# A two-layer hybrid decoder in one kernel: six of the 22 gate/up pairs of each half FFN as whole products, the others as block products of an input that already holds 1/rms

## The chip, the cores and the metric

The kernel runs on one core of a Trainium2 chip. The metric is the device time of one execution in microseconds (us), the median of the runs that are given. TensorE (PE) does the matrix products, VectorE (DVE) and ScalarE (ACT) the element work, GpSimd (POOL) some of it, and the queue of SyncE (SP) issues nearly all transfers.

## The reference

Two layers over 512 tokens of width 1024, all in float32. Each layer is a half FFN, a mixer and another half FFN; the mixers (layer 0: latent attention and gated linear attention, layer 1: sparse attention) are not touched here. There are thus four half FFNs:

```
def rms_norm(x, g):
    y = xf * lax.rsqrt(jnp.mean(xf * xf, axis=-1, keepdims=True) + NORM_EPS)
    return (y * g.astype(jnp.float32)).astype(x.dtype)

def swiglu(x, w_gate, w_up, w_down):
    return (jax.nn.silu(x @ w_gate) * (x @ w_up)) @ w_down

h = h + 0.5 * swiglu(rms_norm(h, ffn_norm[layer, 0]), ffn_w_gate[layer, 0], ffn_w_up[layer, 0], ffn_w_down[layer, 0])
```

The hidden width is 2816, that is 22 blocks of 128. For each block one **pair** is to be made: 128 rows of the gate product and 128 rows of the up product, both over all 1024 input channels and 512 tokens.

## The kernel before

**Layout.** The residual lies transposed in SBUF as eight tiles `x0` to `x7` (the order listings call them x_79 to x_86), 128 channels by 512 tokens each. Every float32 operand of a product is split into a rounded high part and a low part (`split`, L149 to L151: a cast on ACT, a subtraction on DVE), and `mm3` (L143) makes a product of three matmuls: high by high, high by low, low by high (lines 145, 146, 147 of the profile, whatever the product).

**A pair by seven block products.** The channels are cut in two halves, the tokens in two halves of `H` = 256, and gate and up are the two row blocks: a 2 by 2 by 2 block product, made in Strassen's manner (Winograd's form) with seven products in place of eight. The price is in sums. `gate_up` (L113) loads the two weight blocks of 128 by 1024, makes four sums of 128 by 512 on DVE (`sa`, `sb`, L130 to L133) and splits the gate block, `sa`, `sb` and half of the up block. `ffn_input` (L254) makes the seven parts of the input once per half FFN: products of `x` with the gain, their sums (`xf`, L274), their high parts (`xh`, on ACT) and low parts (`xl`, L269, L279, L151 on DVE). 1/rms of each token is not in them. `gate_up_steps` (L302) issues the seven products as a generator, each 4 channel blocks by 3 matmuls of 256 columns, 84 matmuls for a pair; in between ACT and DVE copy and add parts out of PSUM. It ends with `done(gt, ut)`, which is `hidden` (L352): DVE multiplies `gt` by the broadcast tile `rb` of 1/rms (L354), GpSimd multiplies `ut` by it (L355), ACT applies Silu (L356), GpSimd makes the product (L357), ACT and DVE split it into `hid`.

**The order of a half FFN.** `ffn_body` (L343) first makes the input parts, then pairs 0 and 1 in step with each other; `rb` is asked for after their third step (`norm_stats`: squares on ACT, sums of the squares on DVE in the first half FFN and on GpSimd in the other three, L215; a matmul over partitions, L178; seven small DVE steps and a square root on ACT; the diagonal `dg`, L182; a matmul that spreads it, L184; a copy to `rb`, L167). Then the pairs follow one another. The down projection is done in groups of 5, 5, 4, 4 and 4 blocks: once a group's `hid` tiles exist, eight `unit`s (L362), one for each block of output channels, load a slice of `wd`, split it, multiply (`ps_d`) and add into `x` (L369). They are dealt out between the pairs of the next group; the last group's units end the half FFN.

**Buffers.** PSUM has 4 banks for gate/up (`gu`), 3 for the down projection and 1 for the statistics. Three raw weight tiles, three high/low pairs `whi`/`wlo` (gate blocks, `wd` slices) and three `shi`/`slo` (the sums) go round. The tag `act` has 14 tiles: the seven input parts, high and low. The tag `hid` has 9.

**What sets the order.** The program is written stage by stage, and a scheduler of the framework with a timing model of its own arranges each engine's instructions; each engine then runs its list in order and waits at its head. `tc.high_priority(AHEAD)` pulls the copies out of PSUM forward.

Of the kernel before, what the change touches and what calls it, by code (L numbers as in the profile page):

```python
# [19 lines left out]
P = 128  # L20
# [5 lines left out]
EPS = 1e-6  # L26
NEG = -1e30
TINY = 1e-30
GROUPS = ((0, 5), (5, 10), (10, 14), (14, 18), (18, 22))
H = T // 2  # L30
AHEAD = 400
HID = 9
# [6 lines left out]
class Core:  # L39


    def __init__(self, ctx, tc, a):
        self.ctx, self.tc, self.nc, self.a = ctx, tc, tc.nc, a
        nc = self.nc
        ep = lambda name, bufs, **k: ctx.enter_context(tc.tile_pool(name=name, bufs=bufs, **k))
        self.cp = ep("const", 1)
        self.xp = ep("resid", 1)
        self.sp = ep("scr", 1)
        self.wp = ep("wts", 1, side="right")
        cp = self.cp  # L50
# [12 lines left out]
        self.load_x(0, 2)  # L63
        nc.sync.dma_start(out=self.gains, in_=a["gains"])
        self.first = self.gate_up(0, 0, parts=2, meanwhile=lambda: self.load_x(2, KC))

    def load_x(self, k0, k1):
        for k in range(k0, k1):
# [34 lines left out]
        self.fws = ExitStack()  # L103
        self.fw = self.fws.enter_context(self.pool("sums", side="right"))

    def wload(self, src, n, keep=None):

        raw = self.raw(src, n)
        hi, lo = keep or self.wparts()
        self.split(raw[:, :n], hi[:, :n], lo[:, :n])  # L110
        return hi, lo

    def gate_up(self, f, j, parts=1, meanwhile=None):  # L113


        V, a = self.nc.vector, self.a
        w = T
        g = self.raw(a["wgu"][f, j, 0], 1024, parts)
        gh, gl = self.wparts()
        for i in range(parts):  # L120
            c = slice(i * 1024 // parts, (i + 1) * 1024 // parts)
            self.split(g[:, c], gh[:, c], gl[:, c])
        if meanwhile:
            meanwhile()
        u = self.raw(a["wgu"][f, j, 1], 1024)
        ah, al = self.sparts()
        bh, bl = self.sparts()
# [123 lines left out]
        pool, n = self.act  # L251
        return pool.tile([P, 4, H], R, name=name, tag="act", bufs=n)

    def ffn_input(self, gi, hp):  # L254


        V, S = self.nc.vector, self.nc.scalar
        parts = [(self.form("xh"), self.form("xl")) for _ in range(7)]
        whole = [hp.tile([P, 4, H], F32, name="xf", tag="hid", bufs=HID) for _ in range(3)]
        b12, t3, t2 = whole  # L260
        gain = lambda k: self.gains[:, gi, k : k + 1]
        block = lambda k, th: self.x[k][:, th * H : th * H + H]

        def scaled(i, kh, th):
            h, l = parts[i]
            for kk in range(4):
                k = 4 * kh + kk
                S.activation(h[:, kk], block(k, th), AF.Copy, scale=gain(k))
                V.scalar_tensor_tensor(out=l[:, kk], in0=block(k, th), scalar=gain(k), in1=f32v(h[:, kk]), op0=ALU.mult, op1=ALU.subtract)  # L269

        def combine(out, kh, th, t, op):
            for kk in range(4):
                k = 4 * kh + kk
                V.scalar_tensor_tensor(out=out[:, kk], in0=block(k, th), scalar=gain(k), in1=t[:, kk], op0=ALU.mult, op1=op)  # L274

        def negated(i, t):
            h, l = parts[i]
            S.activation(h, t, AF.Copy, scale=-1.0)  # L278
            V.scalar_tensor_tensor(out=l, in0=t, scalar=-1.0, in1=f32v(h), op0=ALU.mult, op1=ALU.subtract)  # L279

        scaled(0, 0, 0)
        for kk in range(4):
            S.activation(b12[:, kk], block(kk, 1), AF.Copy, scale=gain(kk))
        scaled(1, 1, 0)
        combine(t3, 1, 1, b12, ALU.subtract)
        self.split(t3, *parts[2])
        combine(t2, 0, 0, t3, ALU.add)
        negated(3, t2)
        combine(t2, 1, 0, t2, ALU.subtract)
        negated(4, t2)  # L290
        combine(b12, 0, 0, b12, ALU.subtract)
        self.split(b12, *parts[5])
        scaled(6, 1, 1)
        return parts

    def product(self, ps, w, x, start=False):

# [4 lines left out]
    def gate_up_steps(self, hp, w, x, done):  # L302
# [20 lines left out]
        with tc.high_priority(AHEAD):  # L323
            S.copy(sw, wv)
            V.tensor_add(gt[:, :H], vv, sa)
        yield
        self.product(wv, w[4], x[4])
        sx = snap("sx")
# [8 lines left out]
            V.scalar_tensor_tensor(out=ut[:, H:], in0=z, scalar=-1.0, in1=sw, op0=ALU.mult, op1=ALU.subtract)  # L337
        self.product(z, w[6], x[6])
        with tc.high_priority(AHEAD):
            S.copy(gt[:, H:], z)  # L340
        done(gt, ut)

    def ffn_body(self, f, gi, hp, meanwhile, fp, out):  # L343
        nc, a = self.nc, self.a
        V, S, G = nc.vector, nc.scalar, nc.gpsimd
        w = {0: self.first or self.gate_up(f, 0)}
        x = self.ffn_input(gi, hp)
        acc = self.sumsq(self.x, fast=True) if self.first else None
        self.first = None
        hid = {}  # L350

        def hidden(j):  # L352
            def done(gt, ut):
                V.tensor_mul(gt, gt, self.rb)  # L354
                G.tensor_mul(ut, ut, self.rb)  # L355
                S.activation(gt, gt, AF.Silu)  # L356
                G.tensor_mul(ut, gt, ut)  # L357
                t = hid[j] = hp.tile([P, 2, T], R, name="hid", tag="hid", bufs=HID)
                self.split(ut, t[:, 0], t[:, 1])
            return done  # L360

        def unit(g, c):  # L362
            j0, j1 = g
# [5 lines left out]
            V.scalar_tensor_tensor(out=self.x[c], in0=ps, scalar=0.5, in1=self.x[c], op0=ALU.mult, op1=ALU.add)  # L369

        def steps(j):
            return self.gate_up_steps(hp, w.pop(j), x, hidden(j))


        w[1] = self.gate_up(f, 1)
        two = [steps(0), steps(1)]
        for n in range(7):
            if n == 3:
                self.rb = self.norm_stats(acc)[1]
            for s in two:  # L380
                next(s, None)
        w[2] = self.gate_up(f, 2)
        cur = steps(2)
        next(cur)
        todo = []
        for j in range(2, JC):
# [3 lines left out]
            if j + 1 < JC:  # L390
                w[j + 1] = self.gate_up(f, j + 1)
            for n in range(5):
                next(cur)
            nxt = None
            if j + 1 < JC:
                nxt = steps(j + 1)
                next(nxt)
            next(cur, None)
            cur = nxt
# [1068 lines left out]
```

## Time and profile before

| | |
|---|---|
| median of 3 runs | 2078.36 us (2077.57 to 2078.96) |
| the profiled execution | 2078.08 us, of which its span, first to last instruction, is 2076.3 us |
| PE | 12798 matmuls, busy 1969.4 us (95% of the span) |
| DVE, ACT, POOL | busy 1630.2 us (79%), 1093.9 us (53%), 478.5 us (23%) |
| transfers | 186.55 MB, 90 GB/s on average |

How to read it. The profile shows one execution. PE's busy time counts every matmul from its start to its modelled end, and matmuls overlap: one of 256 columns is shown as 0.28 us long, though the next one starts after 0.12 us. A PE that is shown as busy is therefore not one at its peak; the start-to-start distance of consecutive rows is what a matmul costs. The windows view cuts the span into stretches and gives for each engine the busy time and, in brackets, the number of instructions; with a tile's name it counts only those that read or write it. The waits view tells for whom an engine stood idle. In the chain view each piece is counted from the moment its predecessor ended, so that a row of it is the occupancy of the engine, not the latency. `PEclk` is the clock granted to PE, in tenths of full speed on the page and as a share in the windows.

### The profile page before, as it was taken

What the parts mean: (1) busy time and instruction counts of PE and PEld (TensorE: products, weight loads), DVE (VectorE), ACT (ScalarE), POOL (GpSimd) and SP (SyncE); (2) the same over time, 40 slices, a digit from 0 to 9 for tenths busy, and PEclk for the clock granted to TensorE, in tenths of its full rate; (3) what the DMA queues carried; (4) which work ended last, traced back from release to release, by engine and by line L of the source; (5) the groups of instructions that cost most, each with busy time, mean ns of one, the idle gap of its engine ahead of it and who ended that gap; (6) DMA issues with size and microseconds to landing.
All of it is one profiled execution on the core that took longest, in us unless ns stands there. A gap on an engine that the chain in (4) does not pass through costs nothing.

```text
span 2076.3 us, 33618 instructions
## 1 busy us (share of the span) xinstructions
PE 1969.4 (95%) x12798; PEld 1782.4 (86%) x12798; DVE 1630.2 (79%) x2725; ACT 1093.9 (53%) x2012; POOL 478.5 (23%) x434
## 2 busy tenths in 40 slices
PE   6899999999988999999889999999899979999997
PEld 6899999898768999998789999888687869999996
DVE  8988776678889877776987777676899879777774
ACT  6544443665675444444554444454488746444443
POOL 0321111201341221112121111221266412211112
PEclk9999999999999999999999999999899989999998
DMA  3233232321321333223232333254400122332231
GB/s 132 95 100 108 96 102 82 108 72 43 91 66 63 103 113 100 96 96 93 72 102 93 106 102 102 72 161 132 123 1 1 33 80 88 99 114 97 97 102 57
DMA packets 71634, 186.55 MB, mean 90 GB/s; under 512 B 9904, under 2 KB 13104, under 8 KB 71472
## 3 DMA queue, kind: packets, MB, share of 16 engines
q1 hardware_dynamic: 71472, 184.41, 28.1%
q8 instruction: 100, 1.64, 0.3%
q14 instruction: 62, 0.51, 0.1%
HBM read 172.84 MB, written 2.10 MB: 84 GB/s over the span
## 4 chain that ended last, share of the span: by engine, by line
PE 74%; DVE 14%; DMA 5%; ACT 3%; issue 3%; POOL 1%; SPq 0%; DVEq 0%; POOLq 0%; ACTq 0%
PE ps_d L145 7%; PE ps_d L146 7%; PE ps_d L147 7%; PE ps_a L145 7%; PE ps_a L147 7%; PE ps_a L146 7%; PE ps_b L145 5%; PE ps_b L146 5%; PE ps_b L147 5%; DMA raw<-wgu 3%; PE ps_p L145 2%; PE ps_p L146 2%; PE ps_p L147 2%; PE ps_pt L567 2%; DVE wlo L151 2%
## 5 line engine op out<-in xcount | busy, mean ns | idle before, releaser
L150 ACT CAST whi<-raw 128x1024 fp32r<-128x1024 f32 (+3 forms) x317 | 257.5, 815 | 328.0 <-DMA raw<-wd 156.7
L151 DVE TENSOR_TENSOR wlo<-raw,whi 128x1024 fp32r<-128x1024 f32 (+3 forms) x317 | 309.6, 978 | 83.0 <-ACT whi L150 81.8
L145 PE MATMUL ps_a<-xh,shi 128*128 128x256 f32 x1056 | 302.6, 287 | 11.4 <-ACT xh L278 7.7
L146 PE MATMUL ps_a<-xl,shi 128*128 128x256 f32 x1056 | 298.6, 283 | 0.0
L147 PE MATMUL ps_a<-xh,slo 128*128 128x256 f32 x1056 | 297.5, 283 | 0.1
L145 PE MATMUL ps_d<-hid,whi 128*128 128x512 f32 x672 | 264.7, 397 | 3.3 <-ACT hid L150 3.2
L357 POOL TENSOR_TENSOR ut<-gt,ut 128x512 f32<-128x512 f32 x88 | 121.5, 1381 | 630.8 <-ACT gt L356 630.7
L146 PE MATMUL ps_d<-hid,whi 128*128 128x512 f32 x672 | 265.2, 395 | 0.0
L147 PE MATMUL ps_d<-hid,wlo 128*128 128x512 f32 x672 | 264.4, 396 | 0.0
L355 POOL TENSOR_TENSOR ut<-ut,rb 128x512 f32<-128x512 f32 x88 | 142.1, 1616 | 509.9 <-DVE ut L337 347.6
L145 PEld LDWEIGHTS ps_a<-xh,shi 128*128 128x128 f32 x1056 | 200.1, 189 | 16.6 <-ACT xh L278 8.0
L146 PEld LDWEIGHTS ps_a<-xl,shi 128*128 128x128 f32 x1056 | 200.4, 190 | 2.1 <-issue 0.7
L147 PEld LDWEIGHTS ps_a<-xh,slo 128*128 128x128 f32 x1056 | 200.1, 190 | 0.4 <-DVE slo L151 0.3
L151 DVE TENSOR_TENSOR hid<-ut,hid 128x512 fp32r<-128x512 f32 x88 | 71.6, 814 | 111.2 <-ACT hid L150 110.7
L145 PEld LDWEIGHTS ps_d<-hid,whi 128*128 128x128 f32 x672 | 125.9, 188 | 31.4 <-ACT hid L150 4.5
L147 PEld LDWEIGHTS ps_d<-hid,wlo 128*128 128x128 f32 x672 | 126.2, 188 | 29.3 <-DVE wlo L151 1.0
L146 PEld LDWEIGHTS ps_d<-hid,whi 128*128 128x128 f32 x672 | 126.2, 188 | 25.0 <-DVE hid L151 0.6
L558 POOL TENSOR_TENSOR pr<-pr,sums 128x128 f32<-128x128 f32 (+3 forms) x160 | 114.3, 746 | 106.7 <-DVE sums L1312 40.8
L151 DVE TENSOR_TENSOR slo<-sb,shi 128x1024 fp32r<-128x1024 f32 x88 | 134.8, 1532 | 5.0 <-ACT shi L150 4.7
L150 ACT CAST shi<-sa 128x1024 fp32r<-128x1024 f32 x88 | 92.5, 1051 | 74.4 <-PE ps_a L146 66.7
L130 DVE TENSOR_TENSOR sa<-raw 128x512 f32<-128x512 f32 x88 | 74.4, 846 | 59.5 <-DMA raw<-wgu 59.0
L145 PE MATMUL ps_a<-xh,whi 128*128 128x256 f32 x352 | 102.9, 293 | 18.1 <-ACT whi L150 10.8
(432 smaller groups left out, 5719.8 us busy)
## 6 DMA issues: line engine op xcount, KB each, us to landing
raw<-wgu SPq DMA_DIRECT2D x175, 512.0 KB, 3.4
raw<-wd SPq DMA_DIRECT2D x96, 256.0 KB, 2.7
raw<-wd SPq DMA_DIRECT2D x64, 320.0 KB, 2.9
raw<-wo SPq DMA_DIRECT2D x32, 256.0 KB, 2.8
raw<-w1t SPq DMA_DIRECT2D x16, 512.0 KB, 4.0
raw<-w0v SPq DMA_DIRECT2D x8, 512.0 KB, 3.4
raw<-w0t SPq DMA_DIRECT2D x6, 512.0 KB, 3.3
rt_s<-rt_f SPq DMA_DIRECT2D x48, 64.0 KB, 2.0
```

The source lines that it names most:

```text
L130: V.tensor_add(av[:, :w], g[:, :w], u[:, :w])
L145: mm(ps, lh, rh, start=start, stop=False, **k)
L146: mm(ps, lh, rl, start=False, stop=False, **k)
L147: mm(ps, ll, rh, start=False, stop=stop, **k)
L150: self.nc.scalar.copy(hi, src)
L151: self.nc.vector.tensor_sub(lo, src, f32v(hi))
L355: G.tensor_mul(ut, ut, self.rb)
L357: G.tensor_mul(ut, gt, ut)
L558: self.nc.gpsimd.tensor_mul(o, o, w[:, qb : qb + 1].to_broadcast([P, n]))
L567: self.nc.tensor.transpose(ps[:, off : off + P], prs[br][:, o : o + P], self.ident)
```

## The change

The first `NP` = 6 pairs of each half FFN are made by whole products, the other 16 by the seven block products as before.

- **Whole pairs.** `whole(j)` loads and splits the gate and the up block as they are, without sums, and multiplies each with all eight channel tiles at 512 columns: 2 by 8 by 3 = 48 matmuls into two banks `ps_gu`. Their input is only the scaled `x`, split (`ffn_input`: for each `x` tile one ACT and one DVE instruction, L264 and L265). DVE multiplies both results by `rb` on their way out of PSUM (L378), ACT applies Silu, DVE makes the product (L359).
- **Block inputs with 1/rms.** `ffn_forms` is a generator that advances once after each whole pair: 16 multiplications of `x` by gain and `rb` (L280), the sums (L289 to L297), and seven splits (`bh`, `bl`). With 1/rms in the input the block pairs need no multiplication by `rb`: `gate_up_steps` applies Silu on ACT directly, and `done` is one DVE product and a split.
- **GpSimd** has no work left in the pairs. It keeps the sums of squares of three of the four half FFNs.
- **Around it.** Groups of 4, 5, 5, 4, 4 in place of 5, 5, 4, 4, 4. At the very start `x0`, the gains and the first gate block in four parts are loaded, then `x1` to `x7`; before, `x0` and `x1`, the gains and the block in two parts came first. The weights of the first block pair are loaded and summed during the last whole pair.

```diff
-GROUPS = ((0, 5), (5, 10), (10, 14), (14, 18), (18, 22))
+GROUPS = ((0, 4), (4, 9), (9, 14), (14, 18), (18, 22))
+NP = 6
...
-        self.load_x(0, 2)
+        self.load_x(0, 1)
         nc.sync.dma_start(out=self.gains, in_=a["gains"])
-        self.first = self.gate_up(0, 0, parts=2, meanwhile=lambda: self.load_x(2, KC))
+        self.first = self.wload(a["wgu"][0, 0, 0], 1024, parts=4)
+        self.load_x(1, KC)
...
+    def ffn_input(self, gi):
...
+        for i in range(KC // 2):
+            h, l = self.form("xh"), self.form("xl")
+            for e in range(2):
+                k = 2 * i + e
+                hv, lv = (t[:, 2 * e : 2 * e + 2].rearrange("p a t -> p (a t)") for t in (h, l))
+                g = self.gains[:, gi, k : k + 1]
+                S.activation(hv, self.x[k], AF.Identity, scale=g)
+                V.scalar_tensor_tensor(out=lv, in0=self.x[k], scalar=g, in1=f32v(hv), op0=ALU.mult, op1=ALU.subtract)
...
+    def ffn_forms(self, gi, hp, parts):
+        b11, b12, b21, b22, t = (hp.tile([P, 4, H], F32, name="xf", tag="hid", bufs=HID) for _ in range(5))
+        for kh, bs in enumerate(((b11, b12), (b21, b22))):
...
+                    V.scalar_tensor_tensor(
+                        out=b[:, kk], in0=self.x[k][:, ts], scalar=self.gains[:, gi, k : k + 1], in1=self.rb[:, ts], op0=ALU.mult, op1=ALU.mult,
+                    )
+            yield
...
+        V.tensor_sub(t, b22, b12)
+        add(b11)
+        yield
+        add(b21)
+        add(t)
+        yield
+        V.scalar_tensor_tensor(out=t, in0=t, scalar=-1.0, in1=b11, op0=ALU.mult, op1=ALU.subtract)
+        V.scalar_tensor_tensor(out=b21, in0=t, scalar=-1.0, in1=b21, op0=ALU.mult, op1=ALU.subtract)
+        V.tensor_sub(b12, b11, b12)
+        yield
+        for b in (t, b21, b12, b22):
+            add(b)
...
             V.tensor_add(gt[:, :H], vv, sa)
+            S.activation(gt[:, :H], gt[:, :H], AF.Silu)
...
-            S.copy(gt[:, H:], z)
+            S.activation(gt[:, H:], z, AF.Silu)
...
-                V.tensor_mul(gt, gt, self.rb)
-                G.tensor_mul(ut, ut, self.rb)
-                S.activation(gt, gt, AF.Silu)
-                G.tensor_mul(ut, gt, ut)
...
+        def done(j, gt, ut):
+            V.tensor_mul(ut, gt, ut)
...
+        def whole(j):
+            pt = []
+            for s in range(2):
+                wh, wl = self.first or self.wload(a["wgu"][f, j, s], 1024, keep=self.sparts() if s else None)
+                self.first = None
+                ps = self.ps("ps_gu", "gu")
+                for k in range(KC):
+                    c = slice(k * P, (k + 1) * P)
+                    self.mm3(ps, wh[:, c], wl[:, c], *xs[k], k == 0, k == KC - 1)
+                pt.append(ps)
+            if self.rb is None:
+                self.rb = self.norm_stats(acc)[1]
+            ts = [hp.tile([P, T], F32, name=n, tag=n, bufs=2) for n in ("gt", "ut")]
+            for s, t in enumerate(ts):
+                V.tensor_mul(t, pt[s], self.rb)
+                if s == 0:
+                    S.activation(t, t, AF.Silu)
+            done(j, *ts)
...
+            if NP <= j + 1 < JC:
                 w[j + 1] = self.gate_up(f, j + 1)
...
+            if j < NP:
+                whole(j)
+                next(making, None)
```

What stands in the engines' lists. The first place is DVE at the start of the second half FFN, where the mixer's last results are still being added into `x` (`x_86` is the last tile). Before:

```order
L151 TENSOR_TENSOR wlo<-raw,whi 128x1024
L526 TENSOR_TENSOR x_86<-ps_p,x_86 128x512
L130 TENSOR_TENSOR sa<-raw 128x512
L131 TENSOR_TENSOR sa<-raw 128x512
L274 SCALAR_TENSOR_TENSOR xf<-x_83,gains,xf 128x256
L274 SCALAR_TENSOR_TENSOR xf<-x_84,gains,xf 128x256
L274 SCALAR_TENSOR_TENSOR xf<-x_85,gains,xf 128x256
L269 SCALAR_TENSOR_TENSOR xl<-x_85,gains,xh 128x256
L274 SCALAR_TENSOR_TENSOR xf<-x_86,gains,xf 128x256
L151 TENSOR_TENSOR slo<-sb,shi 128x1024
L269 SCALAR_TENSOR_TENSOR xl<-x_86,gains,xh 128x256
```

Now, at the same place:

```order
L151 TENSOR_TENSOR slo<-raw,shi 128x1024
L151 TENSOR_TENSOR wlo<-raw,whi 128x1024
L265 SCALAR_TENSOR_TENSOR xl<-x_85,gains,xh 128x512
L544 TENSOR_TENSOR x_86<-ps_p,x_86 128x512
L151 TENSOR_TENSOR slo<-raw,shi 128x1024
L265 SCALAR_TENSOR_TENSOR xl<-x_86,gains,xh 128x512
L151 TENSOR_TENSOR wlo<-raw,whi 128x1024
L215 TENSOR_TENSOR ssq<-ssq,sq 128x512
```

The sums of weights and of input blocks that stood between the last add into `x` and the last input part are gone; one weight split and one input instruction are left behind the last add.

The second place is DVE in the first half FFN, where 1/rms is made (`rs_q`, `rc`: its small steps; `dg`: the diagonal that a matmul spreads). Before:

```order
L199 RECIPROCAL rc<-rs_q 128x4
L130 TENSOR_TENSOR sa<-raw 128x512
L131 TENSOR_TENSOR sa<-raw 128x512
L200 TENSOR_TENSOR rs_q<-rc 128x4
L132 TENSOR_TENSOR sb<-sa,raw 128x512
L201 TENSOR_TENSOR rs_q<-rs_q,rs_v 128x4
L133 TENSOR_TENSOR sb<-sb,raw 128x512
L202 TENSOR_SCALAR rs_q<-rs_q 128x4
L151 TENSOR_TENSOR wlo<-raw,whi 128x1024
L203 TENSOR_TENSOR rc<-rc,rs_q 128x4
```

Now:

```order
L197 TENSOR_SCALAR rs_v<-ps_s 128x4
L199 RECIPROCAL rc<-rs_q 128x4
L200 TENSOR_TENSOR rs_q<-rc 128x4
L201 TENSOR_TENSOR rs_q<-rs_q,rs_v 128x4
L202 TENSOR_SCALAR rs_q<-rs_q 128x4
L203 TENSOR_TENSOR rc<-rc,rs_q 128x4
L182 TENSOR_SCALAR dg<-ident,rc 128x128 x4
L151 TENSOR_TENSOR slo<-raw,shi 128x1024
L378 TENSOR_TENSOR gt<-ps_gu,rb 128x512
L378 TENSOR_TENSOR ut<-ps_gu,rb 128x512
```

The small steps stand together, and a weight split stands between them and the first multiplication that empties a `ps_gu` bank.

The third place is PE in the first half FFN, where the spreading matmul L184 stands; pair 2, whose gate product follows it, needs the bank of pair 0's gate. Before, L184 stood among block products:

```order
L147 MATMUL ps_a<-xh,wlo 128x256
L145 MATMUL ps_a<-xh,shi 128x256
L146 MATMUL ps_a<-xl,shi 128x256
L184 MATMUL ps_b<-dg,ones 128x512
L145 MATMUL ps_a<-xh,shi 128x256
```

Now:

```order
L146 MATMUL ps_gu<-xl,shi 128x512
L147 MATMUL ps_gu<-xh,slo 128x512
L184 MATMUL ps_b<-dg,ones 128x512
L145 MATMUL ps_gu<-xh,whi 128x512
L146 MATMUL ps_gu<-xl,whi 128x512
L147 MATMUL ps_gu<-xh,wlo 128x512
```

Nothing is left on PE between L184 and pair 2 in the first half FFN; in the second and third, 13 matmuls of pair 1 stand there, in the fourth 32.

More of the change, by code (lines that the diff above doesn't have):

```diff
@@ L104, in open_sums, with wload, gate_up @@
         self.fw = self.fws.enter_context(self.pool("sums", side="right"))
[L106 to L108 removed]
+    def wload(self, src, n, parts=1, keep=None):
+        raw = self.raw(src, n, parts)
         hi, lo = keep or self.wparts()
[L110 removed]
+        for i in range(parts):
+            c = slice(i * n // parts, (i + 1) * n // parts)
+            self.split(raw[:, c], hi[:, c], lo[:, c])
         return hi, lo
[L113 removed]
+    def gate_up(self, f, j):
         V, a = self.nc.vector, self.a
         w = T
[L118 removed]
+        g = self.raw(a["wgu"][f, j, 0], 1024)
         gh, gl = self.wparts()
[L120 to L124, printed above, removed]
+        self.split(g, gh, gl)
         u = self.raw(a["wgu"][f, j, 1], 1024)
@@ L252, in form @@
         return pool.tile([P, 4, H], R, name=name, tag="act", bufs=n)
-    def ffn_input(self, gi, hp):
+    def ffn_input(self, gi):
         V, S = self.nc.vector, self.nc.scalar
[L258 to L294, printed above, removed]
@@ new lines, in ffn_input, with add @@
+        return xs
+    def ffn_forms(self, gi, hp, parts):
+        V = self.nc.vector
+        b11, b12, b21, b22, t = (hp.tile([P, 4, H], F32, name="xf", tag="hid", bufs=HID) for _ in range(5))
+        for kh, bs in enumerate(((b11, b12), (b21, b22))):
+            for th, b in enumerate(bs):
+                for kk in range(4):
+                    k = 4 * kh + kk
+                    ts = slice(th * H, th * H + H)
+                    V.scalar_tensor_tensor(
+                        out=b[:, kk], in0=self.x[k][:, ts], scalar=self.gains[:, gi, k : k + 1], in1=self.rb[:, ts], op0=ALU.mult, op1=ALU.mult,
+                    )
+            yield
+        def add(b):
+            parts.append((self.form("bh"), self.form("bl")))
+            self.split(b, *parts[-1])
+        V.tensor_sub(t, b22, b12)
[10 more added lines that the diff above has]
+            add(b)
@@ L371, in steps @@
         def steps(j):
[L372 to L386, printed above, removed]
+            return self.gate_up_steps(hp, w.pop(j), forms, lambda gt, ut: done(j, gt, ut))
+        making = self.ffn_forms(gi, hp, forms)
+        cur = None
+        for j in range(JC):
             g = next(i for i, (j0, j1) in enumerate(GROUPS) if j0 <= j < j1)
@@ L389, in ffn_body @@
                 todo += [(GROUPS[g - 1], c) for c in range(KC)]
-            if j + 1 < JC:
+            if NP <= j + 1 < JC:
                 w[j + 1] = self.gate_up(f, j + 1)
[L392 to L399, printed above, removed]
+            if j < NP:
+                whole(j)
+                next(making, None)
+                if j == NP - 1:
+                    cur = steps(NP)
+                    next(cur)
+            else:
+                for n in range(5):
+                    next(cur)
+                nxt = None
+                if j + 1 < JC:
+                    nxt = steps(j + 1)
+                    next(nxt)
+                next(cur, None)
+                cur = nxt
             if j == 3 and meanwhile:
```

18 lines of the change are left out of this document (8 added, 10 removed).

## Prediction

> **What bounds the kernel now.** First the page's busy row and two slice rows, then PE's rows in a steady stretch, then the windows view, once for all and once for `ps_d` (the down projection's matmuls).
>
> ```profile
> PE 1969.4 (95%) x12798; PEld 1782.4 (86%) x12798; DVE 1630.2 (79%) x2725; ACT 1093.9 (53%) x2012; POOL 478.5 (23%) x434
> PE   6899999999988999999889999999899979999997
> PEclk9999999999999999999999999999899989999998
> ```
>
> ```profile
> 799.96 0.28 PE L145 MATMUL ps_a<-xh,shi 128*128 128x256 f32 x1
> 804.27 0.28 PE L147 MATMUL ps_a<-xh,slo 128*128 128x256 f32 x1
> ...
> 949.74 0.39 PE L145 MATMUL ps_d<-hid,whi 128*128 128x512 f32 x1
> 953.00 0.40 PE L147 MATMUL ps_d<-hid,wlo 128*128 128x512 f32 x1
> ```
>
> From 799.96 to 804.27 there are 36 narrow starts: 0.120 us each. From 949.74 to 953.00 there are 14 wide ones: 0.233 us. These are the prices of PE; a whole column costs about the same in both.
>
> ```profile
> 0.00:110.00 110.00, 85.70 (x581) 80.24 (x582) 97.28 (x156) 63.59 (x105) 18.67 (x17) 0.94 0.33 107
> 110.00:360.00 250.00, 249.84 (x1701) 231.04 (x1700) 186.53 (x258) 112.17 (x186) 45.99 (x33) 1.00 0.31 100
> 613.70:720.00 106.30, 93.42 (x655) 87.31 (x655) 95.21 (x141) 58.60 (x95) 24.35 (x14) 0.94 0.27 87
> 962.70:1080.00 117.30, 100.43 (x649) 91.30 (x648) 105.15 (x158) 68.51 (x111) 27.50 (x18) 0.93 0.26 85
> 1689.00:1822.00 133.00, 120.91 (x843) 113.41 (x842) 117.56 (x171) 70.64 (x118) 29.45 (x17) 0.94 0.28 90
> ```
>
> ```profile
> 0.00:110.00 110.00, 7.50 (x30) 5.43 (x30) 0.28 (x1) 0.94 0.33 107
> 110.00:360.00 250.00, 100.08 (x405) 73.48 (x405) 20.84 (x32) 1.00 0.31 100
> 613.70:720.00 106.30, 14.12 (x56) 10.28 (x57) 1.38 (x3) 0.94 0.27 87
> 962.70:1080.00 117.30, 26.81 (x110) 19.93 (x110) 5.36 (x8) 0.93 0.26 85
> 1689.00:1822.00 133.00, 24.49 (x99) 18.03 (x100) 4.07 (x6) 0.94 0.28 90
> ```
>
> Columns: PE, PEld, DVE, ACT, POOL with counts, then clock and transfers; the lower five rows are `ps_d`'s. In 110 to 360, 405 wide and 1296 narrow matmuls make 94.4 + 155.5 = 249.9 us of 250: once a half FFN runs, PE is the bound to the last tenth. The other four windows hold the starts of the four half FFNs. Their work is 66.1 + 7.0 = 73.1, 71.9 + 13.0 = 84.9, 64.7 + 25.6 = 90.3 and 89.3 + 23.1 = 112.4 us; the losses are 36.9, 21.4, 27.0 and 20.6, together 105.9 us. What PE waits for there:
>
> ```profile
> PE ps_a L145 <- ACT whi L150: 10.8, 2, 7.6
> ...
> PE ps_a L145 <- DVE x L526: 6.7, 1, 6.7
> ...
> PE ps_b L145 <- DVE gt L325: 5.4, 1, 5.4
> PE ps_a L145 <- ACT xh L278: 5.3, 1, 5.3
> PE ps_a L147 <- DVE wlo L151: 3.7, 1, 3.7
> ...
> PE ps_a L146 <- DVE xl L269: 5.9, 1, 5.9
> ```
>
> Input parts, weight splits and `x` itself, all behind a full DVE (95.2 of 106.3 us in the second start). The starts are bound by DVE, the rest by PE.
>
> **The change part by part.**
>
> *PE in the six pairs.* A whole pair is 48 wide matmuls, 48 x 0.233 = 11.18 us; a block pair 84 narrow ones, 84 x 0.120 = 10.08. That adds 1.10 us to 24 pairs: **+26.4 us**, all on the path, for PE is the bound. The other groups of the down projection make as many matmuls as before: nothing. The Trainium skill speaks against the edit here: Perfetto Trace Analysis, Identifying the Most-Contended Engine, has one improve the engine with the highest occupancy first, and this gives that engine more. By that rule alone the time would be 2078.1 + 26.4 = 2104.5; the trace agrees in 110 to 360 and not in the four starts.
>
> *DVE in the starts.* Its steps, from the chain view:
>
> ```profile
> 28.42 1.59 DVE xf L274 x4
> 32.07 1.14 DVE slo L151
> 33.21 1.14 DVE wlo L151
> 34.34 1.14 DVE xl L279
> 35.48 0.60 DVE sb L132
> 37.82 1.58 DVE xl L269 x4
> ```
>
> ```profile
> L226 DVE SCALAR_TENSOR_TENSOR xl<-x,gains,xh x16: 733/740/1794, 373.6 to 1361.3; 128x512 fp32r<-128x512 f32 x16
> ```
>
> Before, the weights of a pair take four sums and four splits, 4 x 0.60 + 3 x 1.14 + 0.60 = 6.4 us, and the input parts 12 x 0.40 + 16 x 0.40 + 4 x 1.14 = 15.8: for pair 0, 22 us of DVE stand against 10 us of PE. After, the input takes eight steps of 512 columns; the mixers have such steps (L226), 0.73 from start to end, of which the start-up overlaps the next step: between the 0.60 of a sum that wide and 0.73 I take 0.66, 5.3 us. A pair's weights take 2 x 1.14. So 7.6 us stand against 11.2, and PE can run from the first product on. The block inputs come later, 16 x 0.40 + 4 x 1.14 + 7 x 1.14 = 18.9 us, beside whole pairs. All that DVE does up to the end of pair 5: 5.3 + 18.9, six pairs of 2.3 + 4 x 0.60 = 28, weights of pair 6 6.4, the statistics 2 by estimate (13 small steps), four units' split and add 4 x 1.2 = 4.8, in sum 65 us. PE has 6 x 11.18 + 48 x 0.233 = 78. DVE would be 83% busy: the cover holds, with 13 us to spare; if it goes, each us short is one on the path (a rival below).
>
> *What is left of the losses.* First start: `x` bounds it. The rows are the issue of `x2` to `x7`, the first matmuls of the first and of the fourth half FFN, the copies to `rb`, and the time from issue to landing.
>
> ```profile
> 3.07 3.08 SPq L69 DMA_DIRECT2D x<-xT x6
> 7.58 0.58 PE L145 MATMUL ps_a<-xh,whi 128*128 128x256 f32 x1 [7.58 <-ACT whi L150]
> 1689.35 0.50 PE L145 MATMUL ps_a<-xh,whi 128*128 128x256 f32 x2
> ```
>
> ```profile
> L167 ACT COPY rb<-ps_b x8: 567/587/588, 54.4 to 1723.1; 128x512 f32<-128x512 f32 x8
> ```
>
> ```profile
> x<-xT SPq DMA_DIRECT2D x8, 256.0 KB, 6.0
> ```
>
> The last `x` is issued at 5.4 to 6.1 and lands 6.0 later, at 12; the new order moves as many bytes, so it lands then too. Its two parts take 1.3, the last matmuls and a backlog from PE's slow clock some 2: the first product ends at 15.5, against 24 x 0.233 = 5.6 us of work. 10 are lost; the 7.58 ahead of the first matmul, then about 6, lie in them. The second block's low part comes 1.1 us late. Then `rb`: no matmul is left between L184 and pair 2, which needs a bank emptied through `rb`; the copy (0.59), a split that stands first on DVE (1.14), the step itself (0.60) and hand-offs make 2.6. Sum 14. In the other starts 13 or 32 matmuls, 3.0 or 7.5 us, cover the 2.6. There the path is the last add into `x`, a split or two, the input step: 3 us after the last projection matmul, while PE has seven channel tiles (21 matmuls, 4.9 us). That would be nothing; but GpSimd's six sums of squares stay, and hold DVE:
>
> ```profile
> 55.62 1.78 DVE L354 TENSOR_TENSOR gt<-gt,rb 128x512 f32<-128x512 f32 x1
> 59.03 2.30 DVE L151 TENSOR_TENSOR slo<-sa,shi 128x1024 fp32r<-128x1024 f32 x1
> ...
> 55.01 3.55 POOL L355 TENSOR_TENSOR ut<-ut,rb 128x512 f32<-128x512 f32 x2 [53.71 <-ACT rb L167]
> ```
>
> Beside GpSimd's work a step of 0.60 takes 1.78 and one of 1.14 takes 2.30, about 1.1 more; six are 6.6 us. I take 3 us left in the second and third start and 5 in the fourth, where the list puts four splits and all adds ahead of the first input step. For waits that I do not see I add 2 per start. Left: 14 + 3 + 3 + 5 + 8 = **33 us** of 105.9. Bounds: 18 (5, 1, 2 after a first start of 10) and 60 (half and more of today's).
>
> The half-rate clock is in this: in 0 to 110 the granted clock is 0.94. TensorE: Matmul & The Clock Gate, Part 1, says in the Trainium skill that PE runs at half rate until it was busy for some 3.4 us. By that the first start would lose 1.7 us to it, an estimate from that page; I have about 2 within the 10, so the sum would move by 0.3.
>
> *GpSimd out of the pairs.* DVE's step per pair on `gt` (L354) becomes the product (L359), both 0.60; GpSimd's two go. In the steady windows PE has no loss to give back: 0 there, hidden behind PE either way; without that cover DVE would gain. At the ends of half FFNs the last pair's chain is on the path:
>
> ```profile
> L145 PE MATMUL ps_d<-hid,whi 128*128 128x512 f32 x672 | 264.7, 397 | 3.3 <-ACT hid L150 3.2
> ```
>
> 3.2 us in all; one engine step of three falls out of it: **-2**. ACT gets less to do, SP as many transfers: 0.
>
> *Sum.* Against the profiled execution's 2078.1 (the median of the runs is 0.3 above): 2078.1 + 26.4 - 105.9 + 33 - 2 = **2029.6 us**, say 2030.
>
> **The rivals.**
>
> *DVE stays the bound of the starts* (0.20). For: it was busy 90% of its starts and never full, since it waits in its queue behind casts and transfers; at 90%, its 65 us and the held 6.6 need 79.5 us where PE has 78, and each further idle stretch counts in full. Against: the order puts the long waits behind PE's need. Price: 7 us in each half FFN, 2030 + 28 = 2058.
>
> *`rb` comes as late as now, and it is slower* (0.06). The four banks hold pairs 0 and 1; pair 2 starts when `rb` exists, so from 2 x 11.2 = 22.4 us after the first matmul every us is lost. Today (L167's first and last row) it comes 46.8 us after the first matmul (7.58) in the first half FFN, 33.8 us after it (1689.35) in the fourth. At 40 in each: 4 x (40 - 22.4) = 70, and 2100. It decides from (2078 - 2030)/4 + 22.4 = 34.4 us on. For: those two rows stand on either side of it, and four squares, sums and splits share DVE and ACT then. Against: in the new lists the small steps stand together, where today's stand between weight sums.
>
> *It does not do what it says* (0.02): the waits of the starts would be for `x` and for transfers, which no form of the product changes. For: the first start waits so up to about 12 us. Against: in the others the waits named are for parts and splits. PE's starts would then end only some 26 us sooner, as much as the wide products take away: within 4 us of 2078.
>
> **How the numbers follow.** The forecast has the other 0.72, with a range of its own from 2030 - 15 to 2030 + 27 (33 us left replaced by 18 and 60). The mixers' lists are arranged anew by the scheduler, some us either way. The range of 8 in 10 is 2010 to 2058: it allows the mixers 5 us below, reaches to the first rival's own figure and leaves the slower cases out. Over 0.2%, about 4 us, is what a measurement can tell: faster 0.92, the same 0.02, slower 0.06.
>
> **What would show it.** In the new profile: the 16 block pairs again at 0.120 a matmul, `ps_gu` at 0.233; losses of the four starts near 16, 5, 5 and 7 by the same count; in the waits view no line of more than 4 us in the last three starts; `rb` 20 to 24 us after the first matmul; DVE steps beside no GpSimd at 0.60 and 1.14. Wrong would be: `ps_gu` waiting for `rb` or L378 for more than 3 us in a half FFN, or DVE with no idle time until pair 7 and PE waiting for `bl`, or wide matmuls further apart than 0.233.

## The result and the profile after

The changed kernel takes 2027.67 us (median of 4 runs, 2027.19 to 2028.24), the kernel before on the same chip 2078.66 us (4 runs): a ratio of 0.9754, with a 95% interval of 0.9737 to 0.9771, which is about 51 us less. The profiled execution took 2027.53 us, of which 2025.8 are its span. The forecast was 2029.6.

The page's busy rows and slice rows of the changed kernel:

```profile
PE 1968.9 (97%) x11934; PEld 1736.3 (86%) x11934; DVE 1500.1 (74%) x2571; ACT 1020.2 (50%) x1850; POOL 213.4 (11%) x258
PE   8999999999989999999999999999899999999997
PEclk9999999999989999999999999999899999999999
```

PE is shown as busy for as long as before, with 864 matmuls fewer (24 pairs x 36): wide ones took the place of narrow ones. DVE has 130 us less to do, POOL 265 less. The first of the 40 slices rose from 6 to 8.

The windows view over stretches that stand as before to the ends of the stages ahead of them (columns as in the prediction), for all, for `ps_d` and for `ps_gu`:

```profile
0.00:100.00 100.00, 89.97 (x394) 71.30 (x395) 80.81 (x129) 53.45 (x74) 0.70 (x6) 1.00 0.41 131
598.50:704.80 106.30, 100.62 (x481) 83.33 (x481) 79.07 (x115) 45.95 (x60) 3.36 (x2) 0.97 0.30 92
945.00:1060.00 115.00, 113.82 (x539) 92.52 (x538) 97.14 (x140) 58.40 (x81) 10.66 (x6) 1.00 0.34 106
1649.30:1782.00 132.70, 128.80 (x684) 110.18 (x684) 100.09 (x148) 59.70 (x86) 2.30 (x2) 0.97 0.30 94
100.00:340.00 240.00, 240.00 (x1648) 222.81 (x1647) 168.04 (x245) 105.11 (x178) 0.00 (x0) 1.00 0.31 98
```

```profile
0.00:100.00 100.00, 11.85 (x48) 8.80 (x48) 2.74 (x4) 1.00 0.41 131
598.50:704.80 106.30, 17.45 (x72) 13.31 (x72) 4.12 (x6) 0.97 0.30 92
945.00:1060.00 115.00, 32.50 (x135) 24.33 (x133) 9.08 (x14) 1.00 0.34 106
1649.30:1782.00 132.70, 23.70 (x96) 17.55 (x96) 5.50 (x8) 0.97 0.30 94
```

```profile
598.50:704.80 106.30, 70.04 (x288) 55.15 (x288) 8.07 (x12) 0.97 0.30 92
```

In each start stand 288 `ps_gu` matmuls. Counted as in the prediction, wide ones at 0.233 and the others at 0.120, the work of the four starts is 85.2, 98.4, 112.5 and 125.5 us, and the losses are 14.8, 7.9, 2.5 and 7.2, together 32.4 us. The forecast had 16, 5, 5 and 7, together 33. Part of what is left, some 20 of the 32 us, is named by the waits view of PE (in each row: who waits, for whom, us in total, times, longest):

```profile
PE ps_gu L145 <- ACT xh L264: 7.5, 3, 3.9
PE ps_gu L145 <- DVE x L544: 5.7, 1, 5.7
PE ps_gu L145 <- ACT whi L150: 5.3, 1, 5.3
...
PE ps_gu L145 <- DVE gt L378: 1.7, 1, 1.7
...
PE ps_d L145 <- ACT hid L150: 0.3, 1, 0.3
```

The last row belongs to the ends of the half FFNs. The same view of the kernel before has for it

```profile
PE ps_d L145 <- ACT hid L150: 6.0, 4, 2.8
```

four waits, one for each half FFN. From the end of one stage's last matmul to that of the next in us, in the timelines of both kernels (the two half FFNs in the middle together):

| stage | before | after | difference |
|---|---|---|---|
| first half FFN, from the span's start | 385.3 | 368.1 | -17.2 |
| mixer of layer 0 | 228.6 | 230.4 | +1.8 |
| second and third half FFN | 742.7 | 717.1 | -25.6 |
| mixer of layer 1 | 332.9 | 333.7 | +0.8 |
| fourth half FFN | 373.9 | 363.4 | -10.4 |
| final norm and store | 13.1 | 13.0 | 0 |

### The profile page after: what moved, and what is told of

It is laid out like the page before. It is cut to its first block, busy times and chain, and to the rows that moved or that the text cites. A ratio compares the mean times of both kernels' runs of the same rounds, so it can differ in the third digit from the quotient of the medians.

```text
span 2025.8 us, 31367 instructions
## 1 busy us (share of the span) xinstructions
PE 1968.9 (97%) x11934; PEld 1736.3 (86%) x11934; DVE 1500.1 (74%) x2571; ACT 1020.2 (50%) x1850; POOL 213.4 (11%) x258
## 4 chain that ended last, share of the span: by engine, by line
PE 85%; DVE 7%; ACT 3%; DMA 2%; issue 2%; SPq 1%; POOL 0%; DVEq 0%; ACTq 0%; POOLq 0%
PE ps_d L145 8%; PE ps_d L146 8%; PE ps_d L147 7%; PE ps_a L145 6%; PE ps_a L147 6%; PE ps_a L146 6%; PE ps_b L145 5%; PE ps_b L147 5%; PE ps_b L146 5%; PE ps_gu L145 4%; PE ps_gu L146 4%; PE ps_gu L147 4%; PE ps_p L145 2%; PE ps_p L146 2%; PE ps_p L147 2%
## 5 line engine op out<-in xcount | busy, mean ns | idle before, releaser
L150 ACT CAST whi<-raw 128x512 fp32r<-128x512 f32 (+4 forms) x319 | 257.7, 811 | 342.0 <-PE ps_d L146 122.1
L151 DVE TENSOR_TENSOR wlo<-raw,whi 128x512 fp32r<-128x512 f32 (+4 forms) x319 | 312.1, 981 | 89.3 <-ACT whi L150 88.4
L145 PE MATMUL ps_d<-hid,whi 128*128 128x512 f32 x672 | 265.2, 398 | 0.0
L145 PE MATMUL ps_a<-bh,shi 128*128 128x256 f32 x768 | 217.0, 283 | 0.0
L146 PE MATMUL ps_a<-bl,shi 128*128 128x256 f32 x768 | 216.4, 282 | 0.0
L147 PE MATMUL ps_a<-bh,slo 128*128 128x256 f32 x768 | 216.1, 281 | 0.0
L145 PEld LDWEIGHTS ps_d<-hid,whi 128*128 128x128 f32 x672 | 126.1, 188 | 26.8 <-ACT whi L150 1.0
L146 PEld LDWEIGHTS ps_a<-bl,shi 128*128 128x128 f32 x768 | 144.7, 188 | 1.2
L145 PEld LDWEIGHTS ps_a<-bh,shi 128*128 128x128 f32 x768 | 144.1, 188 | 1.2
L147 PEld LDWEIGHTS ps_a<-bh,slo 128*128 128x128 f32 x768 | 145.1, 189 | 0.0
L390 DVE SCALAR_TENSOR_TENSOR x<-ps_d,x 128x512 f32<-128x512 f32 x152 | 104.1, 687 | 43.9 <-PE ps_d L147 43.5
L557 ACT ACTIVATE pr<-sm_s,sm_m 128x512 f32<-128x512 f32 (+3 forms) x160 | 90.3, 566 | 18.9 <-DVE sm_m L553 14.8
```

Source lines behind the costliest of these rows:

```text
L145: mm(ps, lh, rh, start=start, stop=False, **k)
L146: mm(ps, lh, rl, start=False, stop=False, **k)
L147: mm(ps, ll, rh, start=False, stop=stop, **k)
L150: self.nc.scalar.copy(hi, src)
L151: self.nc.vector.tensor_sub(lo, src, f32v(hi))
L557: nc.scalar.activation(p, s[:, :n], AF.Exp, bias=mn, scale=-1.0, accum_out=sums)
```

## The experiments

The theory under test is that of the forecast, called the start theory: the gain is PE's waiting at the starts, which goes since few DVE steps stand ahead of the first products. Its rivals: DVE freed from GpSimd's work (the GpSimd theory), and the block pairs' freedom from `rb` (the 1/rms theory). All ratios are to the kernel before on the same chip, whose median lay between 2078.6 and 2080.6 us; 0.001 is 2.1 us. No run undoes the whole pairs alone, the new order of loads at the very start, or the new groups: with the new order the first matmul starts at 5.30 in place of 7.58, and what that gives of the first half FFN's 17.2 us was not measured.

### GpSimd alone, out and in

The kernel before without GpSimd in the pairs:

```
-                G.tensor_mul(ut, ut, self.rb)
+                V.tensor_mul(ut, ut, self.rb)
...
-                G.tensor_mul(ut, gt, ut)
+                V.tensor_mul(ut, gt, ut)
```

> The kernel before, with GpSimd's two products of each pair given to DVE and nothing else changed. Start theory (the gain of the change comes from PE's waits in the starts of the half FFNs): the steady stretches have no loss to give back, the starts keep their sums and splits on DVE and get 2 x 0.60 us more per pair, the ends of the half FFNs lose an engine step of three; 2072 to 2082 us, 2077 likeliest. GpSimd theory (the gain is DVE freed from GpSimd's work, about 1.1 us on each step that it held, through the whole kernel): at least half of the 51 us, so 2053 us or less.

Measured: 2068.85 us, ratio 0.9947 (0.9931 to 0.9963), 9.7 us less than before. That is outside what either theory gave; it is a fifth of the gain. The groups view of that kernel shows the ends of the half FFNs:

```profile
L145 PE MATMUL ps_d<-hid,whi 128*128 128x512 f32 x672 | 264.4, 395 | 0.8 <-ACT hid L150 0.8
L145 PE MATMUL ps_d<-hid,keep 128*128 128x256 f32 x64 | 18.8, 300 | 2.2 <-ACT hid L150 2.2
```

3.0 us of wait there in place of 6.0. The stages that shrank most are the second half FFN (5.4 us) and the fourth (3.2). In the other direction, the changed kernel with its product on GpSimd:

```
         def done(j, gt, ut):
-            V.tensor_mul(ut, gt, ut)
+            nc.gpsimd.tensor_mul(ut, gt, ut)
```

> The changed kernel with the product of each pair (L359) on GpSimd again. Start theory: one engine hand-off and a slower product return at the end of each half FFN (1 to 2 us each) and GpSimd holds some DVE steps while the block inputs are made, where DVE has 13 us to spare by the forecast; 2030 to 2038 us. GpSimd theory: most of the 51 us is lost again, 2050 us or more.

Measured: 2038.87 us, ratio 0.9802 (0.9783 to 0.9821), some 10 us more than the changed kernel and just above the start theory's range. Both edits agree, though the first takes two products out of each pair and this one puts one back: GpSimd in the pairs costs about 10 us, much less than the GpSimd theory wants and more than the start theory gave. The profiled execution of this kernel took 2042.87 us, 4 more than the median, and the two mixers, which the edit leaves alone, are 5.6 us longer in it; its stages are read with that in mind. At the ends of the half FFNs PE waits in it

```profile
PE ps_d L145 <- ACT hid L150: 2.5, 4, 1.5
```

against 0.3 in the changed kernel. The timeline of this kernel in the first half FFN, where the block pairs begin, shows another way in which it may cost (in brackets the engine's idle time and what ended it):

```profile
95.31 3.27 POOL L359 TENSOR_TENSOR ut<-gt,ut 128x512 f32<-128x512 f32 x1 [17.59 <-DVE ut L378]
...
98.61 0.62 ACT L150 CAST hid<-ut 128x512 fp32r<-128x512 f32 x1 [2.96 <-POOL ut L359]
...
99.13 1.05 ACT L150 CAST whi<-raw 128x1024 fp32r<-128x1024 f32 x1
...
101.74 0.39 PE L147 MATMUL ps_a<-bh,wlo 128*128 128x256 f32 x1 [0.75 <-DVE wlo L151]
...
106.16 0.38 PE L145 MATMUL ps_b<-bh,uhi 128*128 128x256 f32 x1 [1.79 <-DVE gt L331]
```

This product takes GpSimd 3.27 us. ACT stands at the head of its list with the cast of `hid` for 2.96 us, and a weight cast stands behind it; PE then waits for a weight part and for an add that reads a bank of PSUM. That these waits follow from ACT's is read from the order of the rows, not tested. The first half FFN of this execution is 6.0 us longer than in the changed kernel.

### 1/rms late

```
-                    V.scalar_tensor_tensor(
-                        out=b[:, kk], in0=self.x[k][:, ts], scalar=self.gains[:, gi, k : k + 1], in1=self.rb[:, ts], op0=ALU.mult, op1=ALU.mult,
-                    )
+                    V.tensor_scalar_mul(out=b[:, kk], in0=self.x[k][:, ts], scalar1=self.gains[:, gi, k : k + 1])
...
         def done(j, gt, ut):
+            if j >= NP:
+                V.tensor_mul(gt, gt, self.rb)
+                V.tensor_mul(ut, ut, self.rb)
+                S.activation(gt, gt, AF.Silu)
             V.tensor_mul(ut, gt, ut)
```

The two Silu in `gate_up_steps` become a copy and nothing, as before.

> The changed kernel with 1/rms out of the block inputs: they are x times gain alone, and the 16 block pairs multiply both halves by rb on DVE ahead of Silu, as before (2 x 0.60 us of DVE more per pair, 77 us in all). Start theory: the whole pairs make the gain, those 77 us lie beside a PE that is full; only the last pair's chain gets two steps longer, 1.2 us in each half FFN: 2028 to 2036 us. 1/rms theory (the gain is that block pairs need no rb): 2050 us or more.

Measured: 2035.1 us, ratio 0.9792 (0.9771 to 0.9813), 8 us more than the changed kernel: the start theory's range. The waits view of PE:

```profile
PE ps_d L145 <- ACT hid L150: 5.5, 4, 2.2
```

Against 0.3 in the changed kernel, 5.2 of the 8 us are the ends of the half FFNs: with `rb` behind the last product, the last pair's chain has its multiplication by `rb` again. DVE's 69 us more (1569.2 busy against 1500.1) cost less than 3 us elsewhere.

### The same work, earlier in DVE's list

On top of the run before:

```
         making = self.ffn_forms(gi, hp, forms)
+        for n in range(5):
+            next(making)
...
                 whole(j)
-                next(making, None)
                 if j == NP - 1:
+                    next(making, None)
```

> The kernel of the run before this one (1/rms out of the block inputs) with three of the seven block inputs and all their sums made ahead of pair 0 in DVE's list, some 14 us of DVE steps (16 of about 0.35, 3 splits and 4 sums of 1.14, most of them ahead of the first products); not a step more in all. Start theory: what counts is how much DVE work stands ahead of the first products; PE has 11 us of pair 0 to cover 8 of its own splits, so 5 to 11 us come back in each start: 20 to 44 us over the run before, 2050 to 2075 us. Rival (only the sums of weights of the first pairs mattered, and the place of the input's steps does not): within 4 us of the run before.

Measured: 2065.88 us, ratio 0.9936 (0.9914 to 0.9957), 31 us more than the run before, with the same instructions. The rows of PE's timeline in the first half FFN in which it had waited, from the sums of squares on:

```profile
41.45 1.87 PE L178 MATMUL ps_s<-inv_dm,ssq 128*128 128x1 f32 x8 [4.31 <-DVE ssq L215]
45.89 2.05 PE L184 MATMUL ps_b<-dg,ones 128*128 128x512 f32 x2 [2.58 <-DVE dg L182]
49.34 0.79 PE L145 MATMUL ps_gu<-xh,whi 128*128 128x512 f32 x1 [1.40 <-DVE gt L379]
```

and the copies to `rb` (duration, then the start of the first and of the last), here and then in the run before:

```profile
L167 ACT COPY rb<-ps_b x8: 567/585/587, 48.0 to 1713.1; 128x512 f32<-128x512 f32 x8
```

```profile
L167 ACT COPY rb<-ps_b x8: 568/586/587, 35.9 to 1677.2; 128x512 f32<-128x512 f32 x8
```

This is the clearest of the runs: some 14 us of DVE steps in each half FFN (the estimate made with the expectation), moved ahead of the first products, give back three fifths of the whole gain. It also shows through which door. In the first half FFN it is less the first products that come late than the sums of squares and the small steps of 1/rms, behind the block inputs on DVE, while all four banks are full. `rb` is copied 12.1 us later, and the first half FFN is 14.1 us longer. The other three are 12.9 us longer in sum; in the third it is again the diagonal of 1/rms that PE stands for, which it does not in the run before:

```profile
1008.43 1.10 PE L184 MATMUL ps_b<-dg,ones 128*128 128x512 f32 x2 [3.13 <-DVE dg L182]
```

That is the rival of the late `rb`, brought about by the order of DVE's steps. The run moves steps of the input; it does not show what the sums of weights, which the whole pairs spare, cost in the same place.

### More and fewer whole pairs

`NP` = 4, 5 and 8 in place of 6; with 4 and 5 the steps of `ffn_forms` advance two at a time where needed.

> The changed kernel with 4 whole pairs in place of 6 in each half FFN, the block inputs' steps closer together so that they are ready after pair 3. The forecast's two terms apart: a whole pair costs 1.10 us more than a block pair, so 8 fewer save 8.8 us; but DVE's work up to the end of pair 3 is 5.3 + 18.9 + 4 x 4.7 + 6.4 + 2 = 51.4 us against 44.6 of PE, so the cover is short by 6.8 us in each half FFN, 27 us. Cover theory: 2040 to 2050 us, 2046 likeliest. Price alone (the block inputs never limit): 2019 us.

> The changed kernel with 5 whole pairs. Price alone: 4 fewer, 4.4 us saved, 2023 us. Cover theory: DVE has 5.3 + 18.9 + 5 x 4.7 + 6.4 + 2 + 2.4 = 58.5 us up to the end of pair 4 against 5 x 11.16 + 5.6 = 61.4 of PE, 95% busy, so with its own waits it is late by 0 to 4 us in each half FFN: 2023 to 2039 us, 2029 likeliest, which is about the same as with 6.

> The changed kernel with 8 whole pairs. Price of 8 more: 8 x 1.10 = 8.8 us, 2036.5 us, if six pairs already cover all of DVE's work (start theory). If the starts with six still wait for DVE, two more pairs give some of it back: 2028 to 2033 us.

Measured: ratios 0.9752 (0.9736 to 0.9769) with 4, 0.9778 (0.9763 to 0.9794) with 5, 0.9791 (0.9776 to 0.9805) with 8, against 0.9754 with 6. With 8 the price shows: 7.7 us more, where 8.8 were expected, and at most 5 if six pairs had left DVE behind. With 4 neither theory holds: the 8.8 us that are saved are lost again, but not 27. Two of PE's waits with 4 that the changed kernel lacks or has shorter make some 5 of them:

```profile
PE ps_gu L145 <- DVE gt L378: 3.9, 1, 3.9
...
PE ps_b L145 <- DVE gt L331: 2.6, 1, 2.6
```

and with 5, in the timeline of DVE in the first half FFN:

```profile
33.01 0.69 DVE L130 TENSOR_TENSOR sa<-raw 128x512 f32<-128x512 f32 x1 [3.98 <-DMA raw<-wgu]
...
35.96 0.15 DVE L197 TENSOR_SCALAR rs_v<-ps_s 128x4 f32<-128x4 f32 x1
...
38.22 0.87 DVE L182 TENSOR_SCALAR dg<-ident,rc 128x128 f32<-128x128 f32 x4
```

With 5 the scheduler put the weight sums of the first block pair ahead of the small steps of 1/rms. DVE stood 4 us at the first of them for a transfer; the diagonal, at 34.3 in the changed kernel, came at 38.2, and the first half FFN is 4.9 us longer. So in these runs fewer whole pairs give nothing, the waits that are named are for DVE's steps around 1/rms and for a first block product, and 4, 5 and 6 lie within 6 us of each other. Another order with 5 was not tried.

### What is left in the second start

The prediction gave PE seven channel tiles to work on there while the last one is added and split. It did not start on them: it stood for 5.7 us. First, the add pulled forward:

```
-            self.nc.vector.tensor_add(self.x[c], ps, self.x[c])
+            with self.tc.high_priority(AHEAD):
+                self.nc.vector.tensor_add(self.x[c], ps, self.x[c])
```

> The changed kernel with the add of the mixers' output projection (L544) pulled forward in DVE's list by the same priority that the copies out of PSUM have. In the changed kernel PE stands 5.7 us in the second start, and the profile names the last of these adds. If the first product waits for that add (it frees a PSUM bank that the half FFN takes over), it starts up to 4.6 us sooner and 8 matmuls at half rate stay: 2021 to 2025 us, 2023 likeliest. If it waits for the input parts of the last channel tile or for weights instead, 2027 to 2029 us.

Measured: ratio 0.9750 (0.9736 to 0.9765). It tells nothing: the scheduler left the splits ahead of the add where they were, and the wait is 5.67 us as before. If the last product of the projection and the first gate product lie in the same PSUM bank, the first gate product has to wait until that add has read it. So the second run gave the projection two more banks in turn:

```
-                self.out_proj(a["wo0"], oh, ol, 0, 4, ("up", "s"))
+                self.out_proj(a["wo0"], oh, ol, 0, 4, ("up", "s", "pt", "pt"))
```

> The changed kernel with the first mixer's output projection using two more PSUM banks in turn, so that its last two products lie in banks that the half FFN gives to the down projection, not in the bank of the first gate product. Order of DVE unchanged around the last adds. Bank theory (the 5.7 us in the second start are the wait for the bank that the last add frees): the first product starts at once and waits later only for the last channel tile; 4 to 5.5 us gained, some of it PE's half rate after the wait: ratio to the kernel before 0.9728 to 0.9736 (2022 to 2024 us where before is 2078.6). Input theory (it waits for input parts or weights, all behind the same DVE): within 2 us of the changed kernel, ratio 0.975 to 0.976.

Measured: 2026.47 us, ratio 0.9737 (0.9724 to 0.9751). By the medians that is 3.5 us of gain, a little under the 4 to 5.5 expected; the interval meets that of the changed kernel, so the time alone would not settle it. The timeline does, first of the changed kernel, DVE then PE, and after it of this one:

```profile
600.50 2.28 DVE L151 TENSOR_TENSOR wlo<-raw,whi 128x1024 fp32r<-128x1024 f32 x1
...
603.38 0.68 DVE L544 TENSOR_TENSOR x<-ps_p,x 128x512 f32<-128x512 f32 x1
...
604.20 0.76 PE L145 MATMUL ps_gu<-xh,whi 128*128 128x512 f32 x1 [5.67 <-DVE x L544]
604.76 0.63 PE L146 MATMUL ps_gu<-xl,whi 128*128 128x512 f32 x1
...
607.32 0.63 PE L146 MATMUL ps_gu<-xl,whi 128*128 128x512 f32 x1
607.75 0.43 PE L147 MATMUL ps_gu<-xh,wlo 128*128 128x512 f32 x1
608.02 0.39 PE L145 MATMUL ps_gu<-xh,whi 128*128 128x512 f32 x1
```

```profile
598.22 0.39 PE L147 MATMUL ps_p<-oh,wlo 128*128 128x512 f32 x1
598.45 0.39 PE L145 MATMUL ps_gu<-xh,whi 128*128 128x512 f32 x1
598.68 0.40 PE L146 MATMUL ps_gu<-xl,whi 128*128 128x512 f32 x1
```

The first gate product now follows the projection without a gap, and the second half FFN is 5.9 us shorter; the third is 3.0 longer in this profile. So in the changed kernel the wait was for the bank, and the matmuls after it, from 604.76 to 607.32, stand 0.43 apart against 0.233 later: PE ran at about half speed after standing still.

Then GpSimd's sums of squares, beside which DVE's splits take longer there:

```
-                (nc.vector if last or fast else nc.gpsimd).tensor_add(acc, acc, sq)
+                (nc.vector if True else nc.gpsimd).tensor_add(acc, acc, sq)
```

> The changed kernel with the sums of squares of the last three half FFNs on DVE too, six steps of 0.60 us each in place of GpSimd's, which hold DVE steps for about 1.1 us each. Held theory (GpSimd's sums delay the second and the fourth start): 2 to 4 us gained, ratio to the kernel before 0.9735 to 0.9745. Load theory (DVE's own list is the limit there, a held step and a step of its own cost about the same): no gain or up to 4 us lost, ratio 0.9752 to 0.9775.

The edit moves 30 such sums, not only the 18 of the three half FFNs: the norms ahead of the two mixers use the same line, six each. Measured: 2025.42 us, ratio 0.9733 (0.9720 to 0.9747), a gain of some 4 us by the medians, with an interval that meets that of the changed kernel. The wait for the bank fell by half; the split ahead of the last add had taken 2.28 beside GpSimd and takes 1.22 here:

```profile
598.25 1.22 DVE L151 TENSOR_TENSOR wlo<-raw,whi 128x1024 fp32r<-128x1024 f32 x1
599.38 0.68 DVE L544 TENSOR_TENSOR x<-ps_p,x 128x512 f32<-128x512 f32 x1
```

```profile
PE ps_gu L145 <- DVE x L544: 2.9, 1, 2.9
```

The gain lies in the second and third half FFN, together 4.8 us shorter than in the changed kernel; the fourth, which the expectation named too, is 0.9 longer.

> Both edits of the two runs before this one together. If the bank and the held steps are two separate waits, the gains add up: 6 to 9 us, ratio to the kernel before 0.971 to 0.9728. If they are one wait seen twice (the held step only mattered because the bank's add stood behind it), no more than the better of the two alone.

Measured: 2020.7 us, ratio 0.9710 (0.9697 to 0.9723): 9 us less than the changed kernel, its interval clear of that one's, and faster than both kernels of this case. The gains add up: 3.5 and 4 us alone.

> The banks and the sums of squares as in the run before, and 4 whole pairs in place of 6. With 4 pairs alone the 8.8 us that fewer wide products save were lost again, in waits for rb and for block inputs. Theory that those waits came from GpSimd's hold on DVE in the starts: with the hold gone the 8.8 us show, ratio to the kernel before 0.966 to 0.968. Theory that DVE's own amount of work is the limit with 4 pairs (3.6 us more of it in three of the starts): no gain over 6 pairs or a loss, ratio 0.9705 to 0.975.

Measured: 2020.79 us, ratio 0.9711 (0.9698 to 0.9725). No gain over 6 pairs: GpSimd's hold on DVE is not what limits 4 pairs. That DVE's own amount of work and its order do is the theory that is left; no run tests it by itself.

## Why the prediction was right

**The price of the whole pairs** was right. In the timeline of the changed kernel

```profile
639.86 0.39 PE L145 MATMUL ps_gu<-xh,shi 128*128 128x512 f32 x1
...
651.76 0.39 PE L145 MATMUL ps_gu<-xh,shi 128*128 128x512 f32 x1
```

are 51 starts apart, 0.233 us each, and the window from 100 to 340 is still full to the last tenth. Two pairs more per half FFN cost 7.7 us, 0.96 a pair by that run against 1.10.

**The losses of the starts** were right in sum (33 forecast, 32.4 measured), and the run with the same work earlier in DVE's list shows that they hang on what stands ahead on DVE, as the prediction said. In the parts two errors met. The third start lost 2.5, not 5. The second lost 7.9: the step that failed is "the path is the last add into `x`, a split or two, the input step: 3 us after the last projection matmul, while PE has seven channel tiles". The row "PE ps_a L145 <- DVE x L526: 6.7" was read as one more wait for input. In the changed kernel the same wait, 5.7, was for a bank, which no channel tile can cover, as the run with other banks showed; the kernel before has the same banks there, though other banks were not tried in it. With 5.7 the sign "no line of more than 4 us in the last three starts" failed too. In the first start the first product ended at 16.7 where the forecast had 15.5. That the sum is right to 1 us is luck in part.

**GpSimd out of the pairs** was the mis-sized term: -2 forecast at the ends of the half FFNs, 5.7 measured. The prediction took 3.2 us to be all that waits there, from one row of the groups view; the fourth half FFN's last group has its `wd` in a tile of another name (`keep`) and so another row, which held 2.8 more. And the whole 6.0 went but for 0.3, since two things left the chain: GpSimd's product became a DVE step, and the multiplications by `rb` went into the input. The prediction's "one engine step of three" counts one. The runs price each by itself: without GpSimd the kernel before waits 3.0 less there, with its product back the changed kernel waits 2.2 more, and with the late `rb` 5.2 more. These shares sum to more than 5.7, and how the gain divides stays open. So of the some 10 us that GpSimd in the pairs costs, 2 to 3 stand at the ends. The rest lies elsewhere in the half FFNs; the one place that was looked at is ACT's list behind the cast of `hid`. In the sum this rest was part of the losses, whose forecast assumed DVE without GpSimd's products.

**The sum.** With the price of the whole pairs as forecast and the other terms as measured: 2078.1 + 26.4 - 105.9 + 32.4 - 5.7 + 2.6 (the mixers) = 2027.9, against 2027.5 of the profiled execution. So the forecast's 2029.6 is right by its mechanism, and its nearness also owes something to errors that cancel: 3.7 us too little gained at the ends, 2.6 of the mixers' new order not counted.

**The cover of DVE.** It held: from each of the last three starts to the last whole product DVE is busy for 62 to 66 us, 65 forecast, and no product of a block pair waits. But the rule behind it, that all of the block inputs must be ready when the last whole pair ends, is too strict. By it, 4 pairs would lose 27 us; some 8 were lost. A block pair takes its seven inputs one after another, over 10 us, so the last splits have that long. This reading fits the run with 4 but was not tried by itself.

**The rivals.** That DVE or `rb` stays the bound did not happen; the run with the same work earlier in DVE's list shows that both were real, and that in the first half FFN they are one: with the steps pushed ahead, `rb` comes 12 us later and PE stands for it. The expectation that `rb` comes 20 to 24 us after the first matmul was wrong for the first half FFN:

```profile
L167 ACT COPY rb<-ps_b x8: 570/586/587, 36.5 to 1672.9; 128x512 f32<-128x512 f32 x8
```

36.5 is 31.2 after the first matmul at 5.3; it cost only 1.7 us, because PE itself came to the end of pair 1 only 30 us after its first matmul, where two pairs take 22.4: 5.8 us had gone in its first product alone. In the fourth half FFN it was 19.7 after the first matmul at 1653.2.

**The clock.** At the second start PE ran at half speed from 604.20 to 607.75, 3.55 us. That agrees with the page of the Trainium skill that the prediction named, TensorE: Matmul & The Clock Gate, Part 1, by which PE needs about 3.4 us of work to get to full speed. In the first start the nine matmuls from 9.50 on took 4.4 us where 2.1 would do at full speed; the prediction had some 2 us for the slow clock there.

## What to carry to other kernels

Where one engine is the bound in the steady part and another at the start of each stage, a dearer form of the work on the first that spares the second can pay at the starts alone; count how many steps stand ahead of the first products and of what empties their banks, not how many there are. Read a wait row for what the instruction needs: a first product whose operands come from ACT, and that waits for a DVE step which reads the bank it is about to write, may be waiting for the bank; here another bank took the wait away, and a shorter list ahead of that step halved it. A chain's wait at the end of a stage can stand in several rows under several tile names, as the 3.2 and the 2.8 us here: sum the waits by what they wait for.

## What the runs showed of the hardware

A product of two 128x512 float32 tiles takes GpSimd 1.27 to 4.39 us, 2.00 in the median of 88 (first row, of the run with GpSimd in the pairs again: shortest, median and longest in ns), while DVE's same step in the changed kernel has a mean of 0.69 (second row):

```profile
L359 POOL TENSOR_TENSOR ut<-gt,ut x88: 1273/1997/4389, 39.2 to 2003.3; 128x512 f32<-128x512 f32 x88
```

```profile
L359 DVE TENSOR_TENSOR ut<-gt,ut 128x512 f32<-128x512 f32 x88 | 60.3, 686 | 17.8 <-ACT gt L347 16.9 <-ACT gt L380 0.4
```

In the place that was looked at, ACT's list stood still for 2.96 us behind the step that needed its result, while DVE's splits beside it took 1.22 us, as they do without GpSimd.
